# A fixed order on TensorE for the end of an encoder's opening, with filling products between its small steps and shorter inverse roots

## The chip, the cores and the metric

The program runs on one core of a Trainium2 chip. Time is device time in microseconds (us) of one execution. The engines run side by side, each through its own list of instructions in order: TensorE (PE in the profile), VectorE (DVE), ScalarE (ACT), GpSimd (POOL), and SyncE (SP), which here only starts transfers. An instruction starts when the one before it on its engine is out of the way and the results it names are there.

## The reference, cut to what matters

The reference is an encoder of two layers on 512 tokens (an 8 x 64 grid) with 1024 features, in float32. The change touches the beginning of the first layer:

```python
hn = rmsnorm(h, norm_mix[0])
z = hn @ w_in                                    # 1440 columns
qa, ka, va, cq, ckv, kr = split(z)               # 512, 128, 128, 384, 256, 32 columns
qa = axial_rope(rmsnorm(qa per head), row, col)  # 8 heads of 64
ka = axial_rope(rmsnorm(ka per head), row, col)  # 2 heads of 64
oa = softmax(qa @ ka.T / 8) @ va                 # 4 query heads share a key head
# cq, ckv, kr feed a second group of 8 heads (low-rank latents)
```

`rmsnorm(x)` is `x / sqrt(mean(x*x) + 1e-6)` times a gain. Both groups' outputs go through one projection, an MLP follows, then a second layer with neighbourhood attention and another MLP, and a last rmsnorm.

## The kernel before

**Layout and products.** Activations are held transposed (features on partitions, 512 tokens along the free axis), in tiles of 128 x 512. Every operand of a large product is split into a high and a low part, and a product takes three matmuls (`mm3`: high x high, high x low, low x high, lines L501 to L503). Weights come in by SP's queue into buffers named `raw` (four of them), ScalarE makes the high part (`whi`, L212), VectorE or GpSimd the low part (`wlo`, L202).

**The opening.** Columns 0 to 768 of `w_in` (queries, keys, values of the first group) are computed as six output tiles m = 0 to 5 in six PSUM banks at once: m = 0 keys, 1 values, 2 to 5 queries (two heads each). The inner dimension is eight tiles k; for k = 0 to 5 all six outputs are fed, the last two k are run output by output, so that each tile ends in turn and its small steps can begin. Meanwhile the squares of the input are summed (`acc`, L517), `compact_r` turns the sums into one number per token, and its inverse root is `r0` (L764).

**Small steps at the end of the opening.** Keys (`ev_ka`): `stat` squares the tile (ACT L593), splits the squares into high (DVE L594) and low (POOL L595), and two matmuls with an indicator matrix sum them per head (PE L596, L597); `stats_to_tok` copies the sums (ACT L572), turns them so that tokens lie on partitions (PE L575), and forms `rsA`, the inverse root (DVE L578 to L582); this is widened (DVE L661), turned back on PE (`bcast_cols`, L530), and multiplied into the rotated keys (DVE L665), which are split into high and low (ACT L669, DVE L670) and copied across partitions by SP (L671). Values (`ev_va`): ACT L675, transposes on PE L678, then four pairs of a high part (ACT L681) and a low part (DVE L682). Queries (`ev_q`): a `stat` for each of the four tiles into one bank, and a copy (ACT L609); then `q_scales` makes `rsQ` and from it `scA`, the factor with which the scores of every head are scaled; `rope_q(0)` rotates and splits the first pair of heads (shuffle L560, POOL L562, DVE L563, L566, ACT L623, DVE L624).

**Inverse roots.** `rsqrt` is a bit trick and three Newton rounds on VectorE: three steps and three times three (L159 to L169).

**Attention.** `attend` goes through 16 heads (eight of each group) times four blocks of 128 queries, 64 blocks in all: `scores` (PE L997), a scaling and a minimum on VectorE (L1001), `exp` on ScalarE (L1003), a reciprocal and a multiplication (DVE L1004, POOL L1005), transposes three blocks later (PE L972, ACT L974, DVE L975) and products with the values (PE L985). After every block `step` runs `fill.run(1.5)`: from a queue of filling work (the rest of `w_in` by L501 to L503, the rotary key, the latents, the second group's queries, keys and values) it takes products until 1.5 us by its own count (0.69 for three matmuls) are used up.

**What sets the order.** The program is recorded in the order of the Python code, and a scheduler then orders each engine's list by its own estimate of times. Around this change nothing overrides it: TensorE's filling products are pulled ahead and put between the small steps where the scheduler sees room. Two PSUM banks named `t` serve all the small steps in turn; the scores have two banks named `s`.

Of the kernel before, what the change touches and what calls it, by code (L numbers as in the profile page):

```python
# [35 lines left out]
def encoder_kernel(ctx: ExitStack, tc: tile.TileContext, ins, out, dbg=None):  # L36
# [140 lines left out]
    def rsqrt(v, n):  # L177
        got = []
        rsqrt_steps(v, n, got.append)
        return got[0]  # L180

# [337 lines left out]
    def compact_r(acc):  # L519
        b = stb()  # L520
        for i in range(4):
            PE.matmul(b[:, i : i + 1], acc[:, i * P : (i + 1) * P], ones[:, 0:1], start=True, stop=True)
        v = tiny(4)
        DVE.tensor_scalar(v, b[:, 0:4], 1.0 / D, EPS, op0=ALU.mult, op1=ALU.add)
        return rsqrt(v, 4)
# [43 lines left out]
    def stats_to_tok(bk, n, name):  # L569

        st = scratch()
        ACT.activation(st[0:n, :], bk[0:n, :], AF.Copy)  # L572
        tb = stb()
        for i in range(4):
            PE.transpose(tb[:, i * n : (i + 1) * n], st[0:n, i * P : (i + 1) * P], ident[0:n, 0:n])  # L575
        v = keep([P, 4 * n], F32, name)
        v3 = v.rearrange("p (i n) -> p i n", i=4)
        DVE.tensor_tensor(v3, tb[:, 0 : 4 * n].rearrange("p (i n) -> p i n", i=4),  # L578
                          r0sq.unsqueeze(2).to_broadcast([P, 4, n]), op=ALU.mult)
        DVE.tensor_scalar(v, v, 1.0, EPS, op0=ALU.mult, op1=ALU.add)  # L580
        y = rsqrt(v, 4 * n)
        DVE.tensor_tensor(v3, y.rearrange("p (i n) -> p i n", i=4),  # L582
                          r0.unsqueeze(2).to_broadcast([P, 4, n]), op=ALU.mult)
        return v3
# [5 lines left out]
    def stat(src, idx, total, lhs, bk, n):  # L590

        sq, hi, lo = scratch(), scratch(F32R), scratch(F32R)
# [3 lines left out]
        PE.matmul(bk[0:n, :], lhs, hi, start=idx == 0, stop=False)  # L596
        PE.matmul(bk[0:n, :], lhs, lo, start=False, stop=idx == total - 1)  # L597
# [9 lines left out]
    def ev_q(t, b):  # L607
        stat(b, t, 4, ind1(t)[:, 0:8], hold["stq"], 8)
        ACT.activation(QS[t // 2].t[:, S * (t % 2) : S * (t % 2) + S], b, AF.Copy, scale=gT[:, 45:46])  # L609
# [41 lines left out]

    def ev_ka(b):
        st = stb()
        stat(b, 0, 1, ind1(4)[:, 8:10], st, 2)
        kg = scratch()
        ACT.activation(kg, b, AF.Copy, scale=gT[:, 46:47])
        rs = stats_to_tok(st, 2, "rsA")
        krot = rope(kg, cosA, sinA, sw16)
        bk = stb()
# [6 lines left out]
        for v in range(2):  # L666
# [4 lines left out]
            SP.dma_start(f32(kt[z : z + 64, :, :]), f32(kt[a : a + 64, :, :]))  # L671

    def ev_va(b):
        vs = scratch()
        ACT.activation(vs, b, AF.Copy)  # L675
        tb = stb()
        for i in range(4):
            PE.transpose(tb[:, i * P : (i + 1) * P], vs[:, i * P : (i + 1) * P], ident)  # L678
        for i in range(4):
# [3 lines left out]
                                     op0=ALU.mult, op1=ALU.subtract)  # L683

# [22 lines left out]
    def q_scales():  # L707
        rs = stats_to_tok(hold["stq"], 8, "rsQ")
# [51 lines left out]
    for m in range(6):  # L760
        for k in (6, 7):
            use_w(k, m)
        if m == 0:
            DVE.tensor_copy(r0, compact_r(acc))  # L764
# [42 lines left out]
    def latents():  # L807
# [4 lines left out]
        sB = stats_to_tok(b, 2, "rsB")  # L812
# [148 lines left out]
    def attend(heads, step):  # L961
# [31 lines left out]
        def scores(h, i):  # L993
            s = sbk()
            pl = h["passes"](i)
            for n, (lh, rh) in enumerate(pl):
                PE.matmul(s, lh, rh, start=n == 0, stop=n == len(pl) - 1)  # L997
# [79 lines left out]
    def step(h, i):  # L1077
# [10 lines left out]
        fill.run(1.5)  # L1088
# [5 lines left out]
    projB(0, False)  # L1094
    attend(all_heads(), step)
# [633 lines left out]
```

## Time and profile before

| what | value |
|---|---|
| median of 3 runs | 1183.46 us (1182.31 to 1184.22) |
| the profiled execution, span on the core | 1184.0 us |
| PE busy | 1160.5 us, 98% |
| DVE busy | 883.2 us, 75% |
| ACT busy | 640.3 us, 54% |
| POOL busy | 526.1 us, 44% |
| granted TensorE clock, mean of the span | 0.994 |

No time of its own is recorded for the profiled execution beside its span; the span is 0.5 us above the median of the runs.

In rows of the timeline the first number is the start in us from the span's start, the second the duration (or the time from the first to the last of "xN" merged instructions), then engine, line, operation, output<-input, shapes; in brackets stands the engine's idle time just before and what ended it. Rows of a table of windows give the window, its length, then for each engine the busy us with the number of instructions, the granted TensorE clock, the share of the transfer engines and GB/s. Matmuls overlap: one is shown as 0.39 us long, while the next starts 0.23 us after it.

### The profile page before, as it was taken

To read this page: it belongs to the slowest core of one execution; us is meant where nothing else is said; L and a number is where in the kernel's file an instruction comes from. 1 tells how busy PE (TensorE), PEld (TensorE's weight loads), DVE (VectorE), ACT (ScalarE), POOL (GpSimd) and SP (SyncE) were. 2 spreads that over 40 slices of the span, in tenths; PEclk is the share of its full clock that TensorE was granted. 3 is DMA by queue.
4 is the path that set the end of the run, shared out by engine and by line. 5 is a ranking of instruction groups with operands and counts; after the bars stand their busy time and mean duration, and the time that the engine had idled before them with its cause. 6 is when DMAs were issued, how large, how long until landed. Compare 5 with 4: busy or idle time off the path is not lost.

```text
span 1184.0 us, 19784 instructions
## 1 busy us (share of the span) xinstructions
PE 1160.5 (98%) x7128; PEld 1021.2 (86%) x7128; DVE 883.2 (75%) x1514; ACT 640.3 (54%) x1081; POOL 526.1 (44%) x662
## 2 busy tenths in 40 slices
PE   9989999999999999999999999999999999999997
PEld 8667778888899899988998998988889989998895
DVE  5788998878967368786884676667996736778975
ACT  4468676664546247562553565555554624666344
POOL 3267343224562377819602232231376625774710
PEclk9999999999999999999999999999999999999998
DMA  7223225212524723225226464433352341322412
GB/s 244 71 54 92 68 78 134 62 56 77 167 86 134 263 70 90 72 90 165 67 72 178 131 184 126 116 112 109 107 165 76 115 134 55 98 64 89 143 36 71
DMA packets 110145, 128.01 MB, mean 108 GB/s; under 512 B 9075, under 2 KB 86816, under 8 KB 110048
## 3 DMA queue, kind: packets, MB, share of 16 engines
q1 hardware_dynamic: 106992, 119.30, 33.5%
q0 software_dynamic: 2304, 6.31, 2.2%
q8 instruction: 56, 0.92, 0.3%
q10 hardware_dynamic: 752, 1.15, 0.3%
q14 instruction: 41, 0.34, 0.1%
HBM read 104.32 MB, written 6.29 MB: 93 GB/s over the span
## 4 chain that ended last, share of the span: by engine, by line
PE 81%; DVE 4%; ACT 1%; issue 1%; POOL 0%; DVEq 0%; ACTq 0%
PE mm L503 8%; PE mm L501 8%; PE mm L502 8%; PE mm L390 4%; PE mm L389 4%; PE mm L388 4%; PE t L388 3%; PE t L389 3%; PE t L390 3%; PE s L502 2%; PE s L503 2%; PE s L501 2%; PE s L390 2%; PE s L388 2%; PE s L389 2%; PE s L997 2%
## 5 line engine op out<-in xcount | busy, mean ns | idle before, releaser
L309 DVE TENSOR_TENSOR wlo<-a,whi 128x896 fp32r<-128x896 f32 x132 | 161.8, 1230 | 83.7 <-ACT whi L308 82.9
L308 ACT ACTIVATE whi<-a 128x896 fp32r<-128x896 f32 x132 | 125.0, 950 | 155.0 <-PE o L502 45.8
L501 PE MATMUL mm<-a,whi 128*128 128x512 f32 x485 | 195.9, 406 | 0.9 <-DVE a L915 0.7
L503 PE MATMUL mm<-a,wlo 128*128 128x512 f32 x485 | 192.1, 397 | 2.5 <-DVE wlo L202 2.5
L502 PE MATMUL mm<-a,whi 128*128 128x512 f32 x485 | 192.5, 397 | 0.1
L202 DVE TENSOR_TENSOR wlo<-raw,whi 128x1024 fp32r<-128x1024 f32 (+4 forms) x117 | 139.3, 1193 | 66.4 <-ACT whi L212 63.9
L212 ACT ACTIVATE whi<-raw 128x1024 fp32r<-128x1024 f32 (+3 forms) x120 | 116.4, 971 | 92.2 <-PE s L502 39.8
L302 POOL TENSOR_TENSOR a<-a 128x128 f32<-128x128 f32 x132 | 85.1, 645 | 173.3 <-DMA a<-in_ffn_w_up_dram 103.9
L303 POOL TENSOR_TENSOR a<-a 128x256 f32<-128x256 f32 x132 | 120.2, 910 | 10.3
L304 POOL TENSOR_TENSOR a<-a 128x128 f32<-128x128 f32 x132 | 115.1, 872 | 10.3
L503 PEld LDWEIGHTS mm<-a,wlo 128*128 128x128 f32 x485 | 91.7, 189 | 23.7 <-DVE wlo L202 3.4
L501 PEld LDWEIGHTS mm<-a,whi 128*128 128x128 f32 x485 | 91.8, 189 | 20.4 <-PE t L972 0.9
L502 PEld LDWEIGHTS mm<-a,whi 128*128 128x128 f32 x485 | 91.9, 190 | 17.4 <-DVE a L545 0.4
L388 PE MATMUL mm<-a,whi 128*128 128x256 f32 x370 | 103.9, 281 | 0.0
L389 PE MATMUL mm<-a,whi 128*128 128x256 f32 x370 | 103.9, 281 | 0.0
L390 PE MATMUL mm<-a,wlo 128*128 128x256 f32 x370 | 103.7, 280 | 0.0
L1005 POOL TENSOR_SCALAR p<-p,ti 128x512 f32<-128x512 f32 x64 | 46.2, 724 | 92.3 <-DVE ti L1004 81.1
L1430 POOL TENSOR_SCALAR p<-p,ti 128x256 f32<-128x256 f32 x64 | 35.6, 567 | 104.8 <-DVE ti L1429 91.8
L388 PE MATMUL t<-a,whi 128*128 128x256 f32 x264 | 74.2, 281 | 0.0
L389 PE MATMUL t<-a,whi 128*128 128x256 f32 x264 | 74.1, 281 | 0.0
L390 PE MATMUL t<-a,wlo 128*128 128x256 f32 x264 | 73.9, 280 | 0.0
L390 PEld LDWEIGHTS mm<-a,wlo 128*128 128x128 f32 x370 | 69.6, 188 | 0.2 <-DVE wlo L309 0.2
(338 smaller groups left out, 3210.8 us busy)
## 6 DMA issues: line engine op xcount, KB each, us to landing
a<-in_ffn_w_up_dram SPq DMA_DIRECT2D x104, 256.0 KB
raw<-in_ffn_w_down_dram SPq DMA_DIRECT2D x46, 512.0 KB
raw<-in_od_w_qkv_dram SPq DMA_DIRECT2D x64, 128.0 KB
a<-in_ffn_w_down_dram SPq DMA_DIRECT2D x28, 256.0 KB
raw<-in_ffn_w_up_dram SPq DMA_DIRECT2D x12, 512.0 KB
raw<-in_ev_w_in_dram SPq DMA_DIRECT2D x12, 384.0 KB
a<-a SPq DMA_DIRECT2D x18, 256.0 KB
bias<-bx SPq DMA_DIRECT2D x16, 256.0 KB
```

Of the source, the lines that this page charges most:

```text
L202: z = lambda: (eng or DVE).tensor_tensor(to, src, f32(high), op=ALU.subtract)
L212: ACT.activation(hi[:, 0:m], raw[:, 0:m], AF.Copy)
L303: POOL.tensor_tensor(r[:, 4:6], r[:, 2:3].to_broadcast([P, 2, P]), r[:, 0:7:6], op=ALU.add)
L304: POOL.tensor_tensor(r[:, 7], r[:, 3], r[:, 5], op=ALU.subtract)
L308: ACT.activation(hi[:, 0:896], raw[:, 128:1024], AF.Copy)
L309: DVE.tensor_tensor(lo[:, 0:896], raw[:, 128:1024], f32(hi[:, 0:896]), op=ALU.subtract)
L388: PE.matmul(o, wh, x[:, 0], start=kp == 0 and n in (0, 1, 3, 5), stop=False, skip_group_check=True)
L389: PE.matmul(o, wh, x[:, 1], start=False, stop=False, skip_group_check=True)
L390: PE.matmul(o, wl, x[:, 0], start=False, stop=kp == self.np - 1, skip_group_check=True)
L501: PE.matmul(o, wh, xh, start=first, stop=False)
L502: PE.matmul(o, wh, xl, start=False, stop=False)
L503: PE.matmul(o, wl, xh, start=False, stop=last)
```

## The change

Four things are done.

1. **A written order on TensorE.** The last two k of the six tiles and all small steps now stand in a function `finish_opening`, which is called under `tc.manual_schedule(engines={PE})`: TensorE's list is exactly the order of the code there. `ev_ka` and `ev_va` become generators, `stat` and `stats_to_tok` return functions (`sums`, `turn`), so that each step can be placed; the sums of the four query tiles are collected in `late`. Each output tile is computed whole before the next. VectorE, ScalarE and GpSimd are still ordered by the scheduler.
2. **Filling products at written places.** `fill.run` with 1.4, 1.4, 0.7 and 4.0 us of products stands around the queries' last sums and ahead of the first scores; the scores of the first four blocks are held in program order; and after each block of the attention 1.2 us of filling work are taken instead of 1.5.
3. **Roots.** The three roots of the opening (`r0`, `rsA`, `rsQ`) go by `rsqrt_root`: a square root on ScalarE, a reciprocal on VectorE and one Newton round, six steps instead of twelve. The root of the latents (`rsB`) keeps the old way.
4. **Buffers.** The high and low parts of the squares, and the copy of the values, lie in slots of their own instead of the shared scratch buffers, since they now live longer.

```diff
+    def rsqrt_root(v, n):
+        root, hv, y, a, y2 = (tiny(n) for _ in range(5))
+        ACT.activation(root, v, AF.Sqrt)
+        DVE.tensor_scalar(hv, v, -0.5, 1.0, op0=ALU.mult, op1=ALU.mult)
+        DVE.reciprocal(y, root)
+        DVE.tensor_tensor(a, y, y, op=ALU.mult)
+        DVE.tensor_tensor(a, a, hv, op=ALU.mult)
+        DVE.scalar_tensor_tensor(y2, a, 1.5, y, op0=ALU.add, op1=ALU.mult)
+        return y2
...
     def stat(src, idx, total, lhs, bk, n):
-        sq, hi, lo = scratch(), scratch(F32R), scratch(F32R)
+        sq, both = scratch(), Slot()
+        hi, lo = both.t[:, 0:S], both.t[:, S:]
         ACT.activation(sq, src, AF.Square)
         DVE.tensor_copy(hi, sq)
         POOL.tensor_tensor(lo, sq, f32(hi), op=ALU.subtract)
-        PE.matmul(bk[0:n, :], lhs, hi, start=idx == 0, stop=False)
-        PE.matmul(bk[0:n, :], lhs, lo, start=False, stop=idx == total - 1)
+
+        def sums():
+            PE.matmul(bk[0:n, :], lhs, hi, start=idx == 0, stop=False)
+            PE.matmul(bk[0:n, :], lhs, lo, start=False, stop=idx == total - 1)
+            both.free()
+
+        return sums
...
     def q_scales():
-        rs = stats_to_tok(hold["stq"], 8, "rsQ")
+        tok = stats_to_tok(hold["stq"], 8, "rsQ", rsqrt_root)
+        fill.run(0.7)
+        rs = tok()
...
-    for m in range(6):
-        for k in (6, 7):
-            use_w(k, m)
-        if m == 0:
-            DVE.tensor_copy(r0, compact_r(acc))
-            DVE.tensor_tensor(r0sq, r0, r0, op=ALU.mult)
-            ev_ka(banks[0])
-        elif m == 1:
-            ev_va(banks[1])
-            hold["stq"] = stb()
-        else:
-            ev_q(m - 2, banks[m])
-    q_scales()
-    rope_q(0)
+    def finish_opening():
+        def tile(m):
+            for k in (6, 7):
+                use_w(k, m)
+        tile(0)
+        DVE.tensor_copy(r0, compact_r(acc, rsqrt_root))
+        DVE.tensor_tensor(r0sq, r0, r0, op=ALU.mult)
+        keys = ev_ka(banks[0])
+        tile(1)
+        values = ev_va(banks[1])
+        next(values)
+        next(keys)
+        tile(2)
+        hold["stq"] = stb()
+        ev_q(0, banks[2])
+        next(keys)
+        rope_q(0)
+        tile(3)
+        ev_q(1, banks[3])
+        next(keys)
+        next(values)
+        tile(4)
+        ev_q(2, banks[4])
+        tile(5)
+        ev_q(3, banks[5])
+        late.pop(0)()
+        next(keys)
+        late.pop(0)()
+        fill.run(1.4)
+        late.pop(0)()
+        fill.run(1.4)
+        late.pop(0)()
+        q_scales()
+        fill.run(4.0)
...
+            held = tc.keep_in_program_order if count[0] < 4 else lambda z: z
             for n, (lh, rh) in enumerate(pl):
-                PE.matmul(s, lh, rh, start=n == 0, stop=n == len(pl) - 1)
+                held(PE.matmul(s, lh, rh, start=n == 0, stop=n == len(pl) - 1))
...
-        fill.run(1.5)
+        fill.run(1.2)
...
-    attend(all_heads(), step)
+    with tc.manual_schedule(engines={mybir.EngineType.PE}):
+        finish_opening()
+    attend(all_heads(), step)
```

Lines of the changed kernel lie 11 to 59 further down: L512 to L514 are the old L501 to L503, L533 the old L522, L541 the old L530, L588 the old L575, L614 and L615 the old L596 and L597, L709 the old L678, L1054 the old L997, L1058 the old L1001.

**TensorE around the sum of the squares.** `mm_134`, `mm_135`, `mm_136` are the banks of keys, values and the first queries; `a_120`, `a_121` the inputs k = 6 and 7; L522 (now L533) turns `acc` into tokens. Before:

```order
L503 MATMUL mm_134<-a_120,wlo_289 128x512
L501 MATMUL mm_135<-a_120,whi_288 128x512
L501 MATMUL mm_134<-a_121,whi_323 128x512
L502 MATMUL mm_135<-a_120,whi_288 128x512
L503 MATMUL mm_135<-a_120,wlo_289 128x512
L501 MATMUL mm_135<-a_121,whi_323 128x512
L501 MATMUL mm_136<-a_120,whi_288 128x512
L502 MATMUL mm_134<-a_121,whi_323 128x512
```

Now:

```order
L514 MATMUL mm_134<-a_120,wlo_289 128x512
L512 MATMUL mm_134<-a_121,whi_323 128x512
L513 MATMUL mm_134<-a_121,whi_323 128x512
L514 MATMUL mm_134<-a_121,wlo_324 128x512
L533 MATMUL t_405<-ones,acc_122 128x1 x4
L512 MATMUL mm_135<-a_120,whi_288 128x512
L513 MATMUL mm_135<-a_120,whi_288 128x512
```

The products of values and first queries, which stood between the keys' products and ahead of the sum of the squares, now stand behind it.

**TensorE around the keys' factors.** L530 (now L541) turns the widened `rsA` back, L678 (now L709) turns the values, L596 and L597 (now L614 and L615) are the two matmuls of a query tile's sums; `mm_643` is the bank of filling products, `o_139` that of the last query tile. Before:

```order
L501 MATMUL mm_643<-a_119,whi_666 128x512
L502 MATMUL mm_643<-a_119,whi_666 128x512
L503 MATMUL mm_643<-a_119,wlo_667 128x512
L530 MATMUL t_479<-cst,sc_480 128x128 x4
L678 MATMUL t_502<-cst,sc_500 128x128 x4
L501 MATMUL mm_644<-a_114,whi_658 128x512
L502 MATMUL mm_644<-a_114,whi_658 128x512
L596 MATMUL t_515<-sc_523,ind 8x512
```

Now:

```order
L512 MATMUL o_139<-a_121,whi_323 128x512
L513 MATMUL o_139<-a_121,whi_323 128x512
L514 MATMUL o_139<-a_121,wlo_324 128x512
L614 MATMUL t_447<-a_449,ind 8x512
L615 MATMUL t_447<-a_449,ind 8x512
L541 MATMUL t_546<-cst,sc_547 128x128 x4
L614 MATMUL t_447<-a_482,ind 8x512
L615 MATMUL t_447<-a_482,ind 8x512
L512 MATMUL mm_563<-a_114,whi_578 128x512
L513 MATMUL mm_563<-a_114,whi_578 128x512
```

Eighteen filling products stood ahead of the keys' factors; now the first of them stands behind, and the last query tile's products with one pair of sums are the last before them. TensorE's list up to the first scores holds 202 large products (L501 to L503) before and 177 now; up to the 40th block it is 330 and 324.

**VectorE ahead of the keys' factors.** L689 (before L661) widens `rsA`; L714 (L682) are the values' low parts, of which the last must have read the bank that L541 writes; L645 (L624) are the low parts of the rotated first queries; L610 (L594) high parts of squares; L213 (L202) a low part of filling weights. Before, the rows from the last Newton round of `rsA` on:

```order
L169 SCALAR_TENSOR_TENSOR ti_470<-ti_467,ti_465 128x8
L582 TENSOR_TENSOR rsA<-ti_470,r_127 128x8
L661 COPY sc_480<-rsA 128x512
L665 TENSOR_TENSOR sc_486<-sc_475,t_479 128x512
L594 CAST sc_523<-sc_522 128x512
```

Now:

```order
L645 TENSOR_TENSOR a_464<-sc_467,a_464 64x512 x2
L186 TENSOR_SCALAR ti_496<-rsA 128x8
L187 RECIPROCAL ti_497<-ti_495 128x8
L714 SCALAR_TENSOR_TENSOR a_131<-t_507,r_127,a_131 128x2x64
L188 TENSOR_TENSOR ti_498<-ti_497 128x8
L610 CAST a_539<-sc_538 128x512
L189 TENSOR_TENSOR ti_498<-ti_498,ti_496 128x8
L190 SCALAR_TENSOR_TENSOR ti_499<-ti_498,ti_497 128x8
L595 TENSOR_TENSOR rsA<-ti_499,r_127 128x8
L689 COPY sc_547<-rsA 128x512
L213 TENSOR_TENSOR wlo_583<-raw_568,whi_582 128x768
L714 SCALAR_TENSOR_TENSOR a_131<-t_507,r_127,a_131 128x2x64
```

The first queries' rotation and low parts, all four casts of the queries' squares and the values' low parts, which stood behind the keys' factors, now stand ahead of them or among them.

More of the change, by code (lines that the diff above doesn't have):

```diff
@@ L517, in sumsq_acc, with compact_r @@
             (eng or POOL).tensor_tensor(acc, acc, sq, op=ALU.add)
-    def compact_r(acc):
+    def compact_r(acc, root=rsqrt):
         b = stb()
@@ L524, in compact_r @@
         DVE.tensor_scalar(v, b[:, 0:4], 1.0 / D, EPS, op0=ALU.mult, op1=ALU.add)
-        return rsqrt(v, 4)
+        return root(v, 4)
     def bcast_cols(col_ap, nparts, bk):
@@ L607, in ev_q @@
     def ev_q(t, b):
-        stat(b, t, 4, ind1(t)[:, 0:8], hold["stq"], 8)
+        late.append(stat(b, t, 4, ind1(t)[:, 0:8], hold["stq"], 8))
         ACT.activation(QS[t // 2].t[:, S * (t % 2) : S * (t % 2) + S], b, AF.Copy, scale=gT[:, 45:46])
@@ L683, in ev_va @@
                                      op0=ALU.mult, op1=ALU.subtract)
+        yield
     def ev_cq(t, b):
```

46 lines of the change are left out of this document (29 added, 17 removed).

## The prediction

> **What bounds the kernel now.** I read the page's head first, then a table of windows over the first 250 us, then TensorE's timeline where that table shows it idle, and last VectorE's and GpSimd's timelines there. TensorE is busy 98% of the span, so the change can act in two ways only: by the time in which PE waits or runs slowly around the end of the opening, and by what it leaves undone for later. The windows (columns PE, PEld, DVE, ACT, POOL, clock, DMA share, GB/s):
>
> ```profile
> 40.00:50.00 10.00, 9.69 (x49) 7.35 (x48) 8.45 (x31) 3.74 (x7) 2.56 (x2) 1.00 0.01 3
> 50.00:60.00 10.00, 7.90 (x36) 4.83 (x34) 7.21 (x19) 5.82 (x13) 3.61 (x3) 1.00 0.41 105
> 60.00:70.00 10.00, 8.36 (x37) 5.72 (x37) 8.93 (x16) 4.32 (x7) 8.67 (x6) 1.00 0.27 72
> 70.00:80.00 10.00, 7.61 (x28) 5.72 (x27) 7.83 (x24) 5.61 (x11) 2.04 (x4) 0.83 0.12 39
> 80.00:120.00 40.00, 38.55 (x228) 30.59 (x227) 34.34 (x85) 35.07 (x79) 31.88 (x36) 1.00 0.30 80
> 120.00:160.00 40.00, 37.87 (x227) 30.22 (x225) 37.46 (x95) 28.61 (x60) 10.85 (x14) 1.00 0.34 82
> 160.00:250.00 90.00, 89.55 (x528) 75.78 (x527) 75.43 (x168) 60.60 (x128) 30.28 (x39) 1.00 0.28 80
> ```
>
> PE is idle 0.31 + 2.10 + 1.64 + 2.39 = 6.44 us from 40 to 80, and 1.45 + 2.13 + 0.45 = 4.03 us from 80 to 250. Eight waits make the first figure, the largest at the keys' factors and the first scores:
>
> ```profile
> 46.64 0.39 PE L501 MATMUL mm<-a,whi 128*128 128x512 f32 x1
> 46.87 0.39 PE L502 MATMUL mm<-a,whi 128*128 128x512 f32 x1
> ...
> 52.05 0.66 PE L530 MATMUL t<-cst,sc 128*128 128x128 f32 x4 [0.52 <-DVE sc L661]
> ...
> 58.65 0.40 PE L597 MATMUL t<-sc,ind 128*8 128x512 f32 x1 [0.79 <-POOL sc L595]
> ...
> 68.95 1.20 PE L997 MATMUL s<-a,a 128*128 128x512 f32 x4 [1.36 <-DVE a L624]
> ...
> 74.61 0.76 PE L997 MATMUL s<-a,a 128*128 128x512 f32 x2 [2.39 <-DVE ti L1001]
> ```
>
> A product starts every 46.87 - 46.64 = 0.23 us but is shown as 0.39, so each wait also hides 0.16 us of a draining array: 8 x 0.16 = 1.3 us. Behind the 2.39 us wait the clock falls (columns PE, clock):
>
> ```profile
> 75.00:75.50 0.50, 0.50 (x3) 0.68 0.00 0
> 75.50:76.00 0.50, 0.50 (x2) 0.50 0.00 0
> ...
> 78.50:79.00 0.50, 0.50 (x3) 0.91 0.00 0
> ```
>
> About 3.4 us at half speed cost 1.7 us. So before loses 6.4 + 1.3 + 1.7 = 9.4 us here. Until then PE waits so little because 202 products fill the gaps; now 177 stand ahead of the first scores, in fixed places.
>
> **The change part by part: the first tile.** PE now takes the keys' six products and the sum of squares one after the other.
>
> ```profile
> 36.93 0.40 PE L503 MATMUL mm<-a,wlo 128*128 128x512 f32 x1
> ...
> 37.46 0.74 DVE L545 SCALAR_TENSOR_TENSOR a<-t,gT,a 128x512 fp32r<-128x512 f32 x1
> ...
> 39.56 0.69 DVE L517 TENSOR_TENSOR acc<-acc,sc 128x512 f32<-128x512 f32 x1 [0.76 <-ACT sc L515]
> ```
>
> The row at 36.93 is the last product of k = 6, the same in both orders. One product follows, and PE stands at 37.39 at L513, which needs the low part that DVE L545 ends at 37.46 + 0.74 = 38.20: 0.8 us idle. Two products later, at 38.66, L533 needs `acc`, which ends at 40.25: 1.6 us. Before, other outputs' products filled both. In return `r0` starts earlier, at 41.2 instead of 41.6.
>
> **TensorE up to the keys' factors.** From 40.25: the sum of squares 0.95, 30 products 6.9, two pairs of sums 0.9, L588 0.34, L709 0.5, and 0.4 as an estimate for a bank that DVE reads late: PE stands at L541 at about 50.3. L541 is behind nothing that could fill: sums, filling products and scores are all queued behind it. It needs the widened `rsA` (L689) and the bank that the last L714 reads.
>
> **VectorE up to the same place.** The rows that price it:
>
> ```profile
> 41.59 0.16 DVE L524 TENSOR_SCALAR ti<-t 128x4 f32<-128x4 f32 x1 [1.00 <-PE t L522]
> ...
> 42.41 1.26 DVE L167 TENSOR_TENSOR ti<-ti,ti 128x4 f32<-128x4 f32 x1
> ...
> 43.79 0.73 DVE L560 STREAM_SHUFFLE sc<-sc 128x512 f32<-128x512 f32 x1
> ...
> 45.35 0.69 DVE L566 TENSOR_TENSOR sc<-sc,sc 128x512 f32<-128x512 f32 x1
> ...
> 46.35 0.16 DVE L167 TENSOR_TENSOR ti<-ti,ti 128x4 f32<-128x4 f32 x1
> 46.55 0.16 DVE L169 SCALAR_TENSOR_TENSOR ti<-ti,ti 128x4 f32<-128x4 f32 x1
> 46.75 0.17 DVE L764 COPY r<-ti 128x4 f32<-128x4 f32 x1
> ...
> 47.94 0.96 DVE L202 TENSOR_TENSOR wlo<-raw,whi 128x768 fp32r<-128x768 f32 x1
> ...
> 51.56 0.43 DVE L661 COPY sc<-rsA 128x512 f32<-128x512 f32 x1
> ...
> 53.35 0.42 DVE L594 CAST sc<-sc 128x512 fp32r<-128x512 f32 x1
> ...
> 56.49 0.35 DVE L682 SCALAR_TENSOR_TENSOR a<-t,r,a 128x128 fp32r<-128x128 f32 x1
> ```
>
> Small steps go at 0.20 us. The new root saves six, about 1.2 us, and adds a visit to ScalarE, for which this row stands:
>
> ```profile
> 4.59 0.20 ACT L1649 ACTIVATE ti<-ones 128x1 f32<-128x1 f32 x1
> ```
>
> With the two hand-overs (0.2 us each as an estimate) it gives back about half of that, so `r0` is ready at about 43.4: from 41.2 two small steps, the root's five on DVE and one on ACT, 1.6 us, the hand-overs and some lock. That square-root table was loaded ahead of the row at 4.59, and exp comes after all roots: no table load is added. Behind `r0` and ahead of the last L714 VectorE's list holds two shuffles 1.5, four rotation steps 2.8, four casts 1.7, two low parts 1.4, the copy 0.4, four L714 1.4, one L213 1.0 and ten small steps 1.7: 11.8 us, or 10.9 where neighbours overlap as in the rows (0.08 each). Alone that ends at 54.3. But VectorE and GpSimd hold each other up:
>
> ```profile
> 42.36 1.29 POOL L562 TENSOR_TENSOR sc<-sc,a 128x512 f32<-128x512 f32 x1 [0.42 <-PE s L502]
> ...
> 54.12 2.34 DVE L670 TENSOR_TENSOR a<-sc,a 64x512 fp32r<-64x512 f32 x2 [0.36 <-ACT a L669]
> ...
> 68.22 0.68 DVE L624 TENSOR_TENSOR a<-sc,a 64x512 fp32r<-64x512 f32 x1
> ...
> 70.13 1.72 DVE L624 TENSOR_TENSOR a<-sc,a 64x512 fp32r<-64x512 f32 x1
> ```
>
> The L167 at 42.41 took 1.26 us beside that GpSimd step and 0.16 without one (46.35). One window of GpSimd alone (busy us and operations, clock, DMA share, GB/s):
>
> ```profile
> 53.90:71.40 17.50, 13.58 (x9) 1.00 0.32 85
> ```
>
> Beside these nine operations eight VectorE rows, the first at 54.12 and the last at 70.13, are longer than their kind elsewhere, like the L624 at 70.13 by 1.72 - 0.68 = 1.04; together 6.2 us, so 0.69 per GpSimd operation. Six of them (four L611, two L573) now fall into this stretch: 4.2 us, bounds 0 and 6 x 1.29 = 7.7. I take the 0.69 because the mix is that of the window. The last L714 ends at 58.5 (54.3 to 62.0), and PE waits 8.2 us at L541 (4.0 to 11.7).
>
> By the Trainium skill, "SBUF — State Buffer", section "Who interferes with whom", the shared port pair is an exclusive lock held for a whole instruction, and the loser fully blocks. By that each GpSimd step would cost its full length, L541 would start at 62.0 and the sum would be 3.5 us higher; the window's 0.69 speaks for half of it.
>
> **Up to the softmax.** From 58.5 PE has work in hand: L541 0.35, six sums 1.4, 33 products 7.6, L588 0.34: first scores at 68.1. The keys' products, split and copy over partitions run beside the 33 products; SP's copies are issued at about 61.5, and the nearest row of the list of transfers with a time (another queue's; KB, median us to landing) puts them at 65:
>
> ```profile
> a<-a POOLq DMA_DIRECT2D x16, 256.0 KB, 3.4
> ```
>
> `scA` comes at about 68, so the first softmax step runs at 68.6:
>
> ```profile
> 73.80 0.75 DVE L1001 CUSTOM_DVE_ANT_0 p<-s,zeros,scA 128x512 f32<-128x512 f32 x1 [0.15 <-DVE scA L710]
> ```
>
> Attention starts 5.2 us earlier, but 25 products x 0.23 = 5.7 us are owed to it. On a bound PE these cancel; only the waits count. SP's later weight loads wait for L213 at 58 to 60 instead of 49; 33 products of cover hide that. The held scores and the buffers of their own cost nothing by themselves; without a slot, a square's parts would hold up ScalarE.
>
> **The sum.** Lost now: 0.8 + 1.6 + 0.4 + 8.2 = 11.0 us idle, four drains 0.6, and one fall of the clock as before, 1.7: 13.3 against 9.4, so +3.9. The smaller portions (1.2) with 25 products more in stock put 147 products between the first block and the 40th instead of 128: 19 x 0.23 = 4.4 us of cover for the 4.0 us idle there. I take 1.8 back (bounds 0 and 4.0), as the first 80 us of it have most of the idle time and the products are spread evenly. Net +2.1: span 1186.1, and as the span stands 0.5 above the median of the runs, 1185.6 against 1183.46.
>
> The Trainium skill, "TensorE: Matmul & The Clock Gate", "What's actually happening", says that the clock halves after an idle window of about 3.4 us that runs freely. The fall after 2.39 us here is shorter than that and so doesn't agree; by the rule an 8 us wait would find the clock low and cost 1.7 to 3.4, up to 1.7 more on the sum.
>
> **Rivals.**
> - Faster. GpSimd's steps fall beside DVE steps that read PSUM or ACT waits, and hold nothing up. L541 starts at 54.3, PE waits 4.0, loses 9.1 instead of 9.4, and the attention's cover takes back all 4.0: 1179 to 1181. The 1.26 us row speaks against it, the six operations' spread over 11 us for it. It decides from an L541 at about 55.
> - Slower. The lock takes all of each GpSimd step: L541 at 62.0, 11.7 us idle, +5.6: 1189.1, with a longer low clock 1190.8. For it the 1.26 row, against it the mean of 0.69. It decides from an L541 at about 59.
> - No effect: the scheduler's own order of VectorE lets PE lose the same 9.4 us elsewhere: 1183.5. The written order forbids the old filling, so this is small.
>
> **How the numbers follow.** The forecast, a wait of some 8 us at L541, has 0.50; its own range is 1183 to 1188.5. The faster rival 0.27, the slower 0.20, no effect 0.03. A measurement can tell about 0.2%, 2.4 us, from no change. Of the forecast's 0.50, 0.25 lies above 1185.8, 0.21 within, 0.04 below 1181.1; of the faster rival 0.25 below. So faster 0.29, same 0.26, slower 0.45. The range 1179.0 to 1190.5 holds both rivals' middles.
>
> **What would show it.** Right: L541 with a wait of 6 to 10 us that DVE L714 or L689 ends, waits of 0.8 and 1.6 at L513 and L533, first scores near 68, the first softmax at 68 to 69, the low clock near 59 to 62 and not at 75, and less idle time from 80 to 250. Wrong: an L541 before 55 or after 60, a wait at the first scores for the keys' copies, or idle time that the attention keeps.

## The result and the profile after

The changed kernel takes 1195.74 us (median, 1192.5 to 1196.49) against 1183.72 for the kernel before: a ratio of 1.0098, 95% interval 1.0082 to 1.0114. It is about 12 us slower; 1185.6 (1179.0 to 1190.5) was forecast. The profiled execution has a span of 1194.7 us, 10.7 more than before.

The table of windows over the stretch shown above, of the kernel after (length, busy us of PE, PEld, DVE, ACT and POOL, clock, DMA share, GB/s):

```profile
40.00:50.00 10.00, 10.00 (x39) 7.92 (x40) 5.24 (x16) 3.00 (x7) 4.66 (x4) 0.69 0.01 2
50.00:60.00 10.00, 2.68 (x11) 1.43 (x10) 9.77 (x19) 6.82 (x15) 6.96 (x5) 0.82 0.00 1
60.00:70.00 10.00, 8.32 (x28) 5.95 (x28) 4.46 (x7) 1.78 (x3) 0.12 (x1) 0.67 0.47 118
70.00:80.00 10.00, 10.00 (x46) 8.09 (x46) 5.15 (x18) 5.38 (x11) 3.05 (x3) 1.00 0.27 79
80.00:120.00 40.00, 39.07 (x229) 32.45 (x227) 32.88 (x77) 32.62 (x72) 27.76 (x32) 1.00 0.31 85
120.00:160.00 40.00, 37.48 (x213) 28.11 (x212) 34.65 (x88) 25.80 (x55) 14.08 (x16) 1.00 0.29 75
160.00:250.00 90.00, 89.49 (x524) 74.86 (x523) 77.40 (x183) 65.64 (x140) 30.95 (x41) 1.00 0.28 77
```

The first row is the surprise: PE is busy for all of its 10 us, and runs 39 matmuls where it ran 49, at a mean clock of 0.69. The second shows the forecast wait. TensorE's timeline of the kernel after, the rows with a wait and the first scores:

```profile
37.52 0.50 PE L513 MATMUL mm<-a,whi 128*128 128x512 f32 x1 [0.61 <-DVE a L556]
...
39.56 1.87 PE L533 MATMUL t<-ones,acc 128*128 128x1 f32 x8 [1.31 <-DVE acc L528]
...
52.73 0.40 PE L614 MATMUL t<-a,ind 128*8 128x512 f32 x1 [0.68 <-DVE rsA L591]
...
61.68 1.09 PE L541 MATMUL t<-cst,sc 128*128 128x128 f32 x4 [8.32 <-DVE a L714]
...
74.02 0.62 PE L1054 MATMUL s<-a,a 128*128 128x512 f32 x2
```

The four waits are those of the forecast, 0.61 + 1.31 + 0.68 + 8.32 = 10.9 us in all against 11.0 forecast. The clock is not. A "fall" of the clock is a stretch in which the granted clock stands at 0.50. These are TensorE's windows of half a microsecond at the beginning and end of two such stretches, with one inside the second (PE busy, clock, DMA share, GB/s):

```profile
39.00:39.50 0.50, 0.00 (x0) 0.78 0.11 37
...
46.00:46.50 0.50, 0.50 (x3) 0.89 0.00 0
...
56.00:56.50 0.50, 0.00 (x0) 0.85 0.00 0
...
61.50:62.00 0.50, 0.32 (x2) 0.50 0.00 0
...
66.50:67.00 0.50, 0.50 (x4) 0.91 0.94 180
```

All windows between are at 0.50: 39.3 to 46.1 and 56.3 to 66.6. In the first PE works for about 6.5 us, in the second from 61.68 on for 4.9; at half speed that loses 3.3 + 2.4 = 5.7 us where 1.7 was forecast. VectorE shows what the first stretch does downstream:

```profile
43.35 0.16 DVE L802 TENSOR_TENSOR r0sq<-r 128x4 f32<-128x4 f32 x1
...
47.25 0.43 DVE L610 CAST a<-sc 128x512 fp32r<-128x512 f32 x1 [3.09 <-ACT sc L609]
...
49.89 1.78 DVE L574 TENSOR_TENSOR sc<-sc,a 128x512 f32<-128x512 f32 x1
...
54.13 2.36 DVE L645 TENSOR_TENSOR a<-sc,a 64x512 fp32r<-64x512 f32 x2
...
59.09 1.31 DVE L689 COPY sc<-rsA 128x512 f32<-128x512 f32 x1
60.33 0.95 DVE L213 TENSOR_TENSOR wlo<-raw,whi 128x768 fp32r<-128x768 f32 x1
61.20 0.34 DVE L714 SCALAR_TENSOR_TENSOR a<-t,r,a 128x128 fp32r<-128x128 f32 x1
```

`r0` is ready at 43.3 as forecast, but the squares of the first queries come late, since PE computes that tile at half speed: VectorE stands idle for 3.09 us, and the last L714 ends at 61.5 instead of 58.5. PE is late by the same 3 us, so the wait at L541 keeps its length.

### The profile page after: what moved, and what is told of

Read it like the earlier page. It is cut to its first block, busy times and chain, and to the rows that moved or that the text cites. A ratio compares the mean times of both kernels' runs of the same rounds, so it can differ in the third digit from the quotient of the medians.

```text
span 1194.7 us, 19740 instructions
## 1 busy us (share of the span) xinstructions
PE 1165.3 (98%) x7128; PEld 1025.3 (86%) x7128; DVE 878.0 (73%) x1493; ACT 641.0 (54%) x1084; POOL 524.6 (44%) x662
## 4 chain that ended last, share of the span: by engine, by line
PE 87%; DVE 7%; ACT 3%; issue 1%; POOL 1%; DMA 0%; DVEq 0%; POOLq 0%; ACTq 0%
PE mm L512 9%; PE mm L513 9%; PE mm L514 9%; PE mm L401 3%; PE mm L399 3%; PE mm L400 3%; PE s L513 3%; PE s L514 3%; PE s L512 3%; PE t L399 2%; PE t L400 2%; PE t L401 2%; PE s L1054 2%; PE o L1041 2%; PE s L400 2%; PE s L399 2%
## 5 line engine op out<-in xcount | busy, mean ns | idle before, releaser
L512 PE MATMUL mm<-a,whi 128*128 128x512 f32 x485 | 199.4, 411 | 1.3 <-DVE a L886 1.1
L514 PE MATMUL mm<-a,wlo 128*128 128x512 f32 x485 | 192.8, 398 | 2.6 <-DVE wlo L213 2.6
L513 PE MATMUL mm<-a,whi 128*128 128x512 f32 x485 | 193.9, 400 | 0.7 <-DVE a L556 0.6
L213 DVE TENSOR_TENSOR wlo<-raw,whi 128x1024 fp32r<-128x1024 f32 (+4 forms) x117 | 138.0, 1182 | 68.5 <-ACT whi L223 68.1
L313 POOL TENSOR_TENSOR a<-a 128x128 f32<-128x128 f32 x132 | 82.9, 628 | 176.7 <-DMA a<-in_ffn_w_up_dram 111.2
L314 POOL TENSOR_TENSOR a<-a 128x256 f32<-128x256 f32 x132 | 126.4, 957 | 10.3
L315 POOL TENSOR_TENSOR a<-a 128x128 f32<-128x128 f32 x132 | 113.9, 863 | 10.3
L514 PEld LDWEIGHTS mm<-a,wlo 128*128 128x128 f32 x485 | 92.5, 191 | 24.1 <-DVE wlo L213 3.0
L512 PEld LDWEIGHTS mm<-a,whi 128*128 128x128 f32 x485 | 92.8, 191 | 21.5 <-DVE a L886 1.8
```

The source lines that it names most:

```text
L213: z = lambda: (eng or DVE).tensor_tensor(to, src, f32(high), op=ALU.subtract)
L314: POOL.tensor_tensor(r[:, 4:6], r[:, 2:3].to_broadcast([P, 2, P]), r[:, 0:7:6], op=ALU.add)
L315: POOL.tensor_tensor(r[:, 7], r[:, 3], r[:, 5], op=ALU.subtract)
L512: PE.matmul(o, wh, xh, start=first, stop=False)
L513: PE.matmul(o, wh, xl, start=False, stop=False)
L514: PE.matmul(o, wl, xh, start=False, stop=last)
```

## The experiments

### The clock by itself

"warm12" adds products of ones into banks that nothing reads, in the two places where PE waits:

```diff
         tile(0)
+        idle_work(6, stb())
         DVE.tensor_copy(r0, compact_r(acc, rsqrt_root))
...
         late.pop(0)()
+        idle_work(30, mmb())
         next(keys)
```

> The changed kernel with products of ones added on TensorE, whose results nothing reads: 6 calls ahead of the sum of squares (L533) and 30 ahead of the keys' factors (L541). They do no work of the kernel and take away no wait. Theory (the clock): the two falls of the clock, which cost 3.3 and 2.4 us, come from the idle time ahead of L533 and L541; with the array busy there both vanish, the waits stay, and the time falls by 5 to 6 us, to about 1190. Rival (the waits alone): the waits decide and the clock only makes them look shorter; the time stays within 1 us of 1195.7.

Measured: 1190.14 us, ratio to before 1.0043 (1.0026 to 1.006), so 5.6 us less than the changed kernel. Its windows (PE busy, clock):

```profile
36.00:40.00 4.00, 3.34 (x19) 1.00 0.25 66
40.00:50.00 10.00, 9.31 (x48) 1.00 0.01 3
50.00:60.00 10.00, 8.36 (x69) 1.00 0.03 3
60.00:70.00 10.00, 10.00 (x47) 1.00 0.51 130
```

The rows of L541 and of the first scores:

```profile
58.97 0.63 PE L541 MATMUL t<-cst,sc 128*128 128x128 f32 x4 [1.64 <-DVE a L714]
...
69.05 0.62 PE L1056 MATMUL s<-a,a 128*128 128x512 f32 x2
```

The clock stays at 1.00, L541 starts at 58.97 (58.5 was the forecast for an undisturbed clock), and the first scores at 69.05 instead of 74.02. The two falls cost 5 to 6 us, and idle time on PE brings them. They are the part of the loss that the forecast had at 1.7.

### The three waits by themselves

"tiles" puts nine products back ahead of the sum of squares; "fillfirst" takes 18 filling products ahead of L541, "tilesfill" does both:

```diff
-        tile(0)
+        use_w(6, 0)
+        use_w(6, 1)
+        use_w(7, 0)
+        use_w(6, 2)
+        use_w(7, 1)
         DVE.tensor_copy(r0, compact_r(acc, rsqrt_root))
...
-        tile(1)
...
-        tile(2)
+        use_w(7, 2)
```

```diff
         late.pop(0)()
+        fill.run(4.1)
         next(keys)
         late.pop(0)()
-        fill.run(1.4)
         late.pop(0)()
-        fill.run(1.4)
         late.pop(0)()
         q_scales()
-        fill.run(4.0)
+        fill.run(2.7)
```

> The changed kernel with nine products of values and first queries put back ahead of the sum of squares, so that it and the low part of k = 7 are waited for less. Theory (idle time and clock): the 1.9 us idle before L533 and the first fall (3.3 us) vanish, VectorE gets the first queries' tile some 3 us earlier, the wait at L541 stays near 8 us: 1190 to 1191. Rival (VectorE alone sets when L541 runs): L541 stays at 61.7 us, its wait grows by what is gained ahead of it, and the time stays within 1 us of 1195.7.

Measured: 1190.69 us, 1.0047 (1.003 to 1.0063), 5.0 less. The first fall is gone, L541 starts 3.4 us earlier and waits 9.44 us, with one fall of 13.7 us around that wait. The rival, by which VectorE holds L541 at 61.7, falls: VectorE had itself waited for the slow PE.

> The changed kernel with 18 filling products (4.1 us) ahead of L541 instead of behind it; the number ahead of the first scores stays. Theory: the wait at L541 falls from 8.3 to about 4 us and the second fall gets shorter or goes: 1189 to 1191.5. Rival (the first scores wait next): sums and keys come no earlier, the 18 products are missing behind L541, and a wait of 4 us stands at the sums of the queries, L588 or the first scores; the time stays within 1 us of 1195.7.

Measured: 1192.86 us, 1.0061 (1.0038 to 1.0085), 2.9 less. L541 waits 4.22 us and starts as late as before (61.10); nothing waits at the sums or the first scores instead, so the rival falls too. Less than the theory's 4.2 to 6.7 us came, and with four runs from 1189.4 to 1194.5 the size is uncertain. The profiled execution still has two falls, of 3.4 us each (from 41.2 and from 61.7).

> The changed kernel with both moves, the nine products ahead of the sum of squares and the 18 filling products ahead of L541. The sum of the two alone (5.0 and 2.9 us off 1195.7) is 1187.8. Theory: with 4.1 us of products the wait at L541 falls from 9.4 us to about 5 and the fall of the clock, which ran through that wait, gets shorter by up to 2 us: 1185.5 to 1188. Rival (the two moves take back the same wait): no better than the first alone, 1190 to 1191.

Measured: 1188.96 us, 1.0031 (1.0018 to 1.0043). The wait is 5.35 us as expected, the time 1 us above the range: against "tiles" alone the 4.1 us of cover brought 1.7.

### What VectorE does ahead of L541

"ropelate" records the rotation of the first queries behind the keys' factors. TensorE's order stays as it is:

```diff
         ev_q(0, banks[2])
         next(keys)
-        rope_q(0)
         tile(3)
...
         late.pop(0)()
         next(keys)
+        rope_q(0)
         late.pop(0)()
```

> The changed kernel with the rotation of the first queries (one shuffle, two steps, two low parts on VectorE, one step on GpSimd) recorded behind the keys' factors instead of ahead of them. Theory (VectorE's work ahead of L689 and the last L714 is what PE waits for): 3.5 us of VectorE and the lock of a GpSimd step go from there, L541 starts 3.5 to 4.5 us earlier, at 57 to 58, and the time falls by 3 to 6 us: 1189.5 to 1192.5. Rival (the rotation is needed by the first scores and waits there instead): L541 earlier, but a wait of the same length ahead of L1054, and the time within 1 us of 1195.7.

Measured: 1186.19 us, 1.0011 (1.0 to 1.0022): 9.5 us less than the changed kernel, where 3 to 6 were expected. TensorE's rows, of this version:

```profile
37.29 0.50 PE L513 MATMUL mm<-a,whi 128*128 128x512 f32 x1 [0.60 <-DVE a L556]
39.34 0.83 PE L533 MATMUL t<-ones,acc 128*128 128x1 f32 x6 [1.31 <-DVE acc L528]
52.94 1.09 PE L541 MATMUL t<-cst,sc 128*128 128x128 f32 x4 [3.68 <-DVE a L714]
```

No wait stands at the first scores, so the rival falls. In this execution the same waits of 0.60 and 1.31 are there, and yet the clock does not fall behind them (1.00 from 38.5 to 52). It falls only at 52.2, for 3.4 us, of which PE works 2.7. Idle time shrinks from 10.9 to 5.6 us (5.3 less), the loss by the clock from 5.7 to 1.4 (4.3 less): 9.6 in all, and the first scores start 9.8 us earlier, at 64.25. The mechanism, VectorE's work ahead of L689 and L714, was right. But that 9.6 meets the 9.5 of the medians is luck: the profiled execution is the fastest of ten (1183.42 us, mean clock 0.996; the median run stands at 0.994), and 3.3 of its 9.6 us are the first fall, which lies ahead of the moved steps; the last section shows why this execution went without it. The move itself accounts for the 5.3 us of idle time and about 1.0 of the second fall. How the remaining 3 us of the median's gain come about was not told apart.

"ropewarm" was to show the rest of the clock in that version, with products of ones in its two waits:

```diff
         tile(0)
+        idle_work(6, stb())
...
         late.pop(0)()
+        idle_work(12, mmb())
         next(keys)
+        rope_q(0)
```

> The changed kernel with the rotation behind the keys' factors, and products of ones, whose results nothing reads, in the two remaining waits (6 calls ahead of L533, 12 ahead of L541). Theory (one fall of the clock is left in most runs of the version without them, granted clock 0.991 to 0.996): no fall before 100 us, every run at 0.996 or above, 1183 to 1184.5 in place of 1186.2. Rival (the clock has no part in what is left): within 1 us of 1186.2, and as wide a spread.

Measured: 1189.45 us, 1.0048 (1.0032 to 1.0064), slower than without them. The reason stands in its timelines of TensorE and ScalarE:

```profile
62.95 0.59 PE L588 MATMUL t<-cst,sc 8*128 8x8 f32 x4 [3.90 <-ACT sc L583]
```

```profile
61.00 1.28 ACT L644 ACTIVATE a<-sc 64x512 fp32r<-64x512 f32 x2 [2.68 <-DVE sc L577]
62.31 0.59 ACT L583 ACTIVATE sc<-t 8x512 f32<-8x512 f32 x1
```

The added products changed the scheduler's order on another engine: ScalarE now has the rotated queries (L644) ahead of the copy of the sums (L583), where "ropelate" has them behind it, and PE waits 3.90 us for that copy at L588, its order being fixed. A fall of 6.8 us begins inside this wait, and PE works for 6.1 us of it. So this run doesn't separate the clock's share in "ropelate"; it shows that a written order on one engine rests on what a scheduler does with the others.

### The order, the roots, the portion

"a_sched" drops the written order and keeps the rest; "a_oldroots" keeps the order and takes the old roots; "b_roots" has the new roots, with the same `rsqrt_root`, in the kernel before:

```diff
-    with tc.manual_schedule(engines={mybir.EngineType.PE}):
-        finish_opening()
+    finish_opening()
```

> The changed kernel without the written order: TensorE's list by the scheduler, everything else as changed. Theory (the written order made the loss): the waits at L513, L533 and L541 shrink to some 2 us in all and both falls of the clock go; the portion of 1.2 stays: 1184 to 1188. Rival (the loss comes from the recorded order of VectorE's and GpSimd's work or the buffers): L541 still waits over 5 us and the time stays above 1193.

Measured: 1187.77 us, 1.0029 (1.0019 to 1.004): the written order costs 8.0 us, and 3.8 are left of the 12. L541 waits 0.51 us; but 1.75 and 1.25 us stand at two sums of queries, and one fall of 3.4 us remains ahead of the first scores. From 36 us to the first scores PE is idle for 3.7 us, against 10.9 in the changed kernel.

```diff
-        tok = stats_to_tok(st, 2, "rsA", rsqrt_root)
+        tok = stats_to_tok(st, 2, "rsA")
...
-        tok = stats_to_tok(hold["stq"], 8, "rsQ", rsqrt_root)
+        tok = stats_to_tok(hold["stq"], 8, "rsQ")
...
-        DVE.tensor_copy(r0, compact_r(acc, rsqrt_root))
+        DVE.tensor_copy(r0, compact_r(acc))
```

> The changed kernel with the old inverse roots in all three places. Theory: each root takes some 0.6 to 1.2 us longer on the path to L541 (two of them lie there), so the wait at L541 grows by 1 to 2.5 us and the time by as much: 1196.5 to 1198.5. Rival (the visits to ScalarE, behind other work in its list, cost what the steps save): within 1 us of 1195.7.

Measured: 1196.55 us, 1.011 (1.0093 to 1.0127), 0.8 more than the changed kernel. The wait at L541 is 10.24 us instead of 8.32, as the theory had it; with spreads of 3 to 4 us the time alone doesn't tell it.

```diff
-        rs = stats_to_tok(st, 2, "rsA")
+        rs = stats_to_tok(st, 2, "rsA", rsqrt_root)
...
-        rs = stats_to_tok(hold["stq"], 8, "rsQ")
+        rs = stats_to_tok(hold["stq"], 8, "rsQ", rsqrt_root)
...
-            DVE.tensor_copy(r0, compact_r(acc))
+            DVE.tensor_copy(r0, compact_r(acc, rsqrt_root))
```

> The kernel before with the three roots alone by ScalarE and one Newton round. By the theory the first softmax step, which waits for the last root, comes 1 to 2 us earlier, the wait of 2.39 us ahead of the third scores shrinks, and the fall of the clock behind it may go: 1 to 4 us faster, 1179.5 to 1182.5. Rival (the visit to ScalarE costs what the steps save): within 1 us of 1183.5.

Measured: 1183.26 us, 0.9988 (0.9974 to 1.0001). The roots bring about 1 us at most, at the edge of what can be told, where 1 to 4 were expected. The first scores start at 65.6 instead of 69.0, and the wait ahead of the third scores is 2.16 us instead of 2.39. In the profiled execution (span 1177.4, the fastest of ten) no fall follows it, though in the kernel before one followed.

The portion after each block was changed alone in the kernel before:

```diff
-        fill.run(1.5)
+        fill.run(1.2)
```

> The kernel before with portions of 1.2 instead of 1.5 us after each block, and nothing else. Theory: the portion is no part of the loss; the opening is untouched and the idle time from 80 to 250 us stays at 4 us or grows by 1 to 2, as less filling work stands between the blocks: 1184 to 1186 against 1184.1. Rival (the smaller portion brings the two waits for VectorE's low parts near 481 and 490 us, 1.2 us together, which the changed kernel shows and the kernel before doesn't): they are here too, and the time is 1 to 2 us longer.

Measured: 1190.58 us, 1.0045 (1.003 to 1.006): 5 to 6 us slower, by a change that the forecast had as a gain. The waits at 481 and 490 aren't here, so the rival falls too. One window from the first score to the first product of the MLP, in the kernel before, in this one and in the changed one; the first two hold the same 1384 matmuls:

```profile
68.95:336.20 267.25, 260.61 (x1384) 212.79 (x1385) 227.96 (x466) 170.82 (x338) 118.92 (x136) 0.99 0.32 92
```

```profile
68.73:341.02 272.29, 263.64 (x1384) 213.27 (x1385) 227.08 (x466) 170.93 (x338) 119.75 (x136) 0.99 0.31 90
```

```profile
74.02:344.35 270.33, 266.15 (x1411) 216.41 (x1410) 222.62 (x456) 172.12 (x340) 120.28 (x138) 1.00 0.31 90
```

With 1.2 the stretch is 5.0 us longer, and only 2.0 of it are idle time (8.65 against 6.64). The other 3.0 are shown as busy, and the clock doesn't make them: each of the two windows holds one fall of 3.4 us. A matmul is shown as 0.39 us long while the next can start 0.23 us after it, so a wait of up to 0.16 us behind it is not shown as idle. Such short waits are the likely reason, though they were not counted one by one: from the start of each transpose (L972) to the start of the next matmul it is 28.0 us in all instead of 23.7.

The other way round, "a_fill15" is the changed kernel with the old portion, "a_sched15" the same without the written order:

```diff
-        fill.run(1.2)
+        fill.run(1.5)
```

> The changed kernel with portions of 1.5 us after each block, as before. The portion of 1.2 alone made the kernel before 6.4 us slower. Theory (the stock pays for the portion): here 25 products more are left for the attention, so 1.2 lost less: its idle time from 80 to 250 us was 4.0 us as in the kernel before; with 1.5 it falls to 2 to 3 us, and the time by 2 to 5 us: 1190.5 to 1193.5. Rival (the portion costs the same in both): 6 us faster, 1189 to 1190. Second rival (the stock only ends sooner): within 1 us of 1195.7.

Measured: 1193.89 us, 1.0088 (1.007 to 1.0107), 1.8 less than the changed kernel, which the overlapping intervals don't tell from no difference. In the written order the portion costs much less than in the kernel before; that the 25 products more in stock are the reason is not shown.

> The changed kernel without the written order and with portions of 1.5 us: roots, buffers and recorded order are left. Theory (the portion makes the 3.8 us): 1183 to 1185. Rival (the recorded order and the buffers make it): within 1 us of 1187.8.

Measured: 1184.79 us, 1.0006 (0.9996 to 1.0017). Without the written order and with 1.5 the changed kernel is as fast as the kernel before. So the portion makes 3.0 of the 3.8 us, and the recorded order and the buffers cost nothing that can be told. In the two profiled executions only 1.2 us of it lie ahead of the MLP, which begins at 334.09 instead of 335.26.

And "b_roots18" is "b_roots" with a larger one:

```diff
-        fill.run(1.5)
+        fill.run(1.8)
```

> The kernel before with the new roots and portions of 1.8 us. Theory (more products beside each block cover more short waits): 1 to 3 us less than the 1183.3 with 1.5: 1180 to 1182.5. Rival (the stock ends before the attention does, and its last blocks lose what the first gain): 1183 to 1187.

Measured: 1188.27 us, 1.0036 (1.0024 to 1.0048), 5.0 slower than with 1.5. The theory that more products beside each block cover more waits falls. The waits from 80 to 160 us sum to 6.6 us in this version (2.6 in "b_roots"), at attention's and at filling's own products alike. The profiled execution, the slowest of ten, also has falls of 3.4 us from 71.7 and of 6.8 us from 143.4, where that of "b_roots" has none; but the clock is not the whole difference, since runs with the same mean clock of 0.995 take 1186.8 to 1188.6 us here and 1183.7 to 1185.1 in "b_roots". Without the written order, then, both directions from 1.5 lose. Why 1.5 is right there was not found.

### The moves together

"best12" has all three moves: the diffs of "tiles" and "fillfirst", and `rope_q(0)` behind the `next(keys)` that follows the 18 products. "best15" has the portion of 1.5 as well.

> The changed kernel with three moves: nine products ahead of the sum of squares, 18 filling products ahead of L541, the rotation behind it. Theory: L541 is reached at about 54 and its data are there at 53 to 55, so no wait over 1.5 us is left before the attention, no fall of the clock, and the opening loses some 7 us less than that of the kernel before; the attention and the MLP take back 1 to 2: 1177 to 1181. Rival (the rotation and the later weights hold up the first scores): a wait of 2 to 4 us at L1054 with a fall behind it, 1183 to 1187.

Measured: 1184.22 us, 0.9997 (0.9987 to 1.0007).

> The three moves (nine products ahead of the sum of squares, 18 ahead of L541, the rotation behind it) with portions of 1.5 us. By the theory of the portion 2 to 5 us less than the 1184.2 with 1.2: 1179 to 1182, which would be faster than the kernel before. Rival (the stock only ends sooner): 1183.5 to 1185.

Measured: 1184.59 us, 1.0003 (0.9993 to 1.0012). Both undo the whole loss and beat nothing. L541 still waits 2.8 us. The first scores start at 64.9 and 63.8, 4 to 5 us ahead of the kernel before, with 18 matmuls (4.1 us) owed; but the stretch from there to the MLP takes 270.2 and 271.4 us, 266.1 and 267.3 without the owed ones, against 263.0 in the kernel before without its wait of 2.39 us and its fall. So the attention loses again what the opening wins, with either portion.

## Why the prediction was wrong, point by point

- **The idle time of the opening** was right: 10.9 against 11.0 us, place by place (0.61 for 0.8, 1.31 for 1.6, 0.68 for 0.4, 8.32 for 8.2). "a_sched" shows that the written order makes it. The 8.32 is no luck of two errors: in "warm12", without the falls, TensorE's own work ends at 50.6 and the last L714 at 58.8, where 50.3 and 58.5 were forecast.
- **The end of the last L714** was put at 58.5 and came at 61.5. So the sign that was to show the forecast wrong, an L541 after 60, is there (61.68), but the clock brought it and not the lock: without the falls ("warm12") L541 ran at 58.97. VectorE's and GpSimd's lock was priced nearly right: six VectorE rows from 47.25 to 60.4 are longer than their kind by 5.1 us in all beside six GpSimd steps (forecast 4.2), as the L574 at 49.89 by 1.1. The full lock that the Trainium skill has in "SBUF — State Buffer", "Who interferes with whom", would have made it 7.7, as an estimate from six steps of 1.29 us; the trace lies between. What was missed are the 3.09 us in which VectorE waits for PE (0.33 in "warm12"). The hand-over to ScalarE, put at 0.2 us as an estimate, took 0.04: VectorE's L535 ends at 41.62 and the root on ScalarE starts at 41.66.
- **The clock, "one fall of the clock as before, 1.7"**, is the first step that failed. There were two falls, of 6.8 and 10.2 us, and 5.7 us lost: 4.0 too little in the sum. The first came behind 1.9 us of waits that the forecast itself had listed and for which it gave no fall; of the five traces that have these two waits unfilled, four show it. The second began inside the 8.32 us wait, and 4.9 us of work ran at half speed behind that. The Trainium skill, "TensorE: Matmul & The Clock Gate", "What's actually happening", has the clock judged by a free-running window of 3.4 us; every fall in these traces that ends before the program does lasts a whole number of such windows (3.4, 6.8, 10.2, 13.7). That a whole idle window is needed doesn't agree: 1.64 us of idle time in the 3.4 us ahead of the first fall sufficed here. The last section counts this over all traces.
- **What the attention gives back, "I take 1.8 back"**, is the second. The stretch from first score to MLP takes 270.33 us instead of 267.25. With the 25 products (5.7 us) taken off the first, and the 2.39 us wait, its 0.16 and its fall (1.7) off the second, it is 264.6 against 263.0: 1.6 lost, not 1.8 won, 3.4 us off. The idle time from 80 to 250 is 3.96 us as before (4.03), so not even that fell. The step counted the products in stock as cover for waits, and they covered none. Why is open. The smaller portion costs 5 to 6 us in the kernel before, but it doesn't explain this stretch: in "a_fill15", with the old portion, it takes 270.66 us, no less. Waits too short to be shown as idle time may stand here as in "b_fill12"; that is not shown.
- **The first softmax step** was forecast at 68.6 and ran at 74.7; the clock accounts for 5 of the 6 us, since "warm12" has its first scores 5.0 us earlier.
- **Beyond 344 us** the loss grows from 8.1 to 10.7 us, which no step had. Half of it are two waits for low parts of weights in the MLP (kernel after):

```profile
481.81 0.39 PE L401 MATMUL s<-a,wlo 128*128 128x256 f32 x1 [0.50 <-DVE wlo L320]
490.26 0.39 PE L401 MATMUL mm<-a,wlo 128*128 128x256 f32 x1 [0.69 <-DVE wlo L320]
```

  They are absent in the kernel before, in "b_roots", "b_fill12", "ropelate" and "best12", and there in part or whole in most other versions; their cause stays open. Near the end each of the two profiled executions also has a fall of 3.4 us, from 1102.6 and from 1114.5; it adds nothing to the difference.
- **Span and median:** the span was taken to stand 0.5 us above the median of the runs. In the runs of these experiments each time stands 1.7 to 2.2 us above its own span, and the spans of the kernel before go from 1179.4 to 1185.5. The profiled execution was a late one of its kind. On the scale of medians that adds 1.3 us to the 10.7.
- **The rivals:** the slower one had the right sign and 1189 to 1191, by a longer wait at L541, which didn't come. Its remark on a longer low clock was the right one, and too small.

The sum, up to the MLP: 2.1 forecast, 4.0 more by the clock and 3.4 by the attention make 9.5, against 8.9 measured there (8.1, and 0.7 by which this execution was ahead at 36 us).

## What to carry to other kernels

Price idle time on a busy TensorE at more than its length: add up what falls into 3.4 us, not only the longest wait, and from about 1.6 us on count the half-speed work that may follow, and what the slower products make late on other engines. Before an engine's order is written by hand, look for instructions that wait for a long chain elsewhere and have everything queued behind them: here one row, L541, held all sums, products and scores. Moving five VectorE steps out of its chain made the median 9.5 of the 12 us better, of which some 6 us are shown to be its own. The size of a portion of filling work belongs to its surroundings: change it alone, and measure it alone, in both directions and in each order of the rest.

## What was not expected of the hardware

- In each trace all falls begin and end on one grid with a step of 3.41 us, to within 3 ns (the last one ends with the program), and the grid lies differently against the program's start from trace to trace. What counts is how much idle time of TensorE one step of the grid holds. Over the 17 traces, from 36 us on and where the clock was full, a fall followed each of the 40 steps with 1.92 us or more of idle time (17 of them at the program's end), none of the 2501 with less than 1.60, and 4 of the 11 between. So a wait that the grid cuts in two can go free. Steps of the grid with PE's busy time, clock, DMA share and GB/s: the one ahead of the fall in the kernel before (2.39 us idle), the two around the first fall of the changed kernel (1.64 us idle, then the fall), the two that share the wait of 2.16 us in "b_roots" (1.30 and 0.96 us idle), and the two that share the 1.9 us in "ropelate" (1.17 and 0.75):

```profile
71.76:75.18 3.42, 1.03 (x6) 1.00 0.03 11
...
35.86:39.28 3.42, 1.78 (x6) 1.00 0.31 77
39.28:42.69 3.41, 3.13 (x11) 0.50 0.00 0
...
65.50:68.92 3.42, 2.12 (x8) 1.00 0.72 230
68.92:72.33 3.41, 2.45 (x10) 1.00 0.00 0
...
35.18:38.59 3.41, 2.24 (x9) 1.00 0.24 55
38.59:42.01 3.42, 2.67 (x16) 1.00 0.06 22
```

- The same shows far from the change: a wait of 1.6 to 2.7 us for a weight's low part stands between 1097 and 1114 us in all 17 traces, and a fall of 3.4 us, worth 1.7, follows it in nine. That fits the spread of 3 to 5 us between runs of one kernel (spans of the changed kernel 1190.7 to 1194.7 with mean clocks of 0.992 to 0.989). So a single execution can't be compared with another within a few us unless the falls are counted in both.
- A fall that begins during a wait goes on behind it: the one at 56.3 began inside the wait at L541 and still took 4.9 us of work at half speed.
- Waits behind a matmul of up to 0.16 us don't appear as idle time (it is shown as 0.39 us, and the next can start after 0.23). With the same 1384 matmuls and the same fall, 3.0 of the 5.0 us lost in "b_fill12" are not shown as idle time, and are probably of this kind.
